# A delta rule's inverse of 16x16 blocks by two blocks of 8 and a product below them

## The chip, the cores and the metric

The kernel runs on one core of a Trainium2 chip. The metric is the device time of one execution of the whole program, in microseconds (us). TensorE is PE in the rows (PEld its weight loads), VectorE is DVE, ScalarE is ACT, GpSimd is POOL, and SyncE (SP) issues the DMAs of the weights.

## The reference, cut to what matters

Two residual blocks run one after the other on 256 tokens of width 1024. The first has two layers; each layer mixes tokens by three linear recurrences (RWKV-7, gated linear attention, gated DeltaNet), with feed-forward networks around them. Two of the three are delta rules, which are computed in chunks of 64 tokens; a chunk needs the inverse of a unit lower triangular 64x64 matrix per head. In the reference of the gated DeltaNet it is seen at once:

```python
decay = jnp.exp(jnp.where(causal, g[..., :, None] - g[..., None, :], -jnp.inf))
kb = k * beta[..., None]
lower = jnp.where(strict, jnp.einsum('bhnid,bhnjd->bhnij', kb, k) * decay, 0.0)
eye = jnp.eye(C, dtype=lower.dtype)
t_inv = lax.linalg.triangular_solve(eye + lower, jnp.broadcast_to(eye, lower.shape),
                                    left_side=True, lower=True)
u = t_inv @ (v * beta[..., None])
w = t_inv @ (kb * jnp.exp(g)[..., None])
```

C is 64, and with 4 heads and 4 chunks there are 16 such matrices. RWKV-7 is written as a scan over tokens, which the kernel computes in chunks of 64 in the same way, with 8 heads and so 32 matrices. `causal` is the lower triangle with its diagonal, `strict` the one without.

## The kernel before

**Weights.** All weights are streamed. A tile of 128x1024 (`wr`) comes by a DMA from SP, ACT casts it to its upper part `wh` (L81, CAST), DVE takes the rest as `wl` (L82), and each product is three passes on PE: L105, L106 and L108 where the output is transposed (128x256 in one pass), L184, L185 and L186 where it isn't (128x512). These passes are called fill below: they don't depend on the delta rules and can stand anywhere between their steps.

**Order.** Each engine runs its instructions in one fixed order, which the scheduler of the language sets when the program is built, from costs that it holds for each instruction; at run time semaphores only make an engine wait. So when an instruction's cost changes in the source, the order of all engines is made anew, and fill may come to stand ahead of a step or behind it.

**The inverse.** It runs four times in an execution: after the projections of RWKV (function `rw_inverse`) and in the middle of the gated DeltaNet (function `gd_mid`), in each of the two layers. The four places are called rw0, gd0, rw1 and gd1 here; they begin at about 285, 401, 1133 and 1249 us of the span. At rw0 and rw1 two groups of 16 matrices are inverted one after the other (two calls of `inv64`), at gd0 and gd1 one group. The steps:

- `inv_put` (L431) copies the 16x16 diagonal blocks of all matrices into a stage `stg`, by ACT (L440) and POOL (L438).
- `inv16` (L442) brings one block of 16x16 to each of the 128 partitions: a transposition on DVE (L449, tile `iA`), then a choice by a mask (L451, L452, tile `ia`). The inverse `ix` starts as the unit matrix and is filled row by row by forward substitution: for i from 1 to 15 a multiplication of i x i elements (L458, tile `ip`) and a sum over one of their axes (L459). Each step needs the one before. Two ACTIVATE on ACT (L462) spread the result, and a transposition (L464, tile `iB`) brings it back.
- `inv64` (L467) copies the blocks to the diagonal of 64x64 matrices, `z0` (tile `iz`), by four copies on ACT (L476, 32x256 elements each). From there it is PE's: inverses of 16 become inverses of 32 and then of 64 by masked products (L496) with DVE and ACT between them (L480, L491, L505, L507, L515, L519). PE's first product of the group, pc<-iz,NT at rw0 and rw1 and pc<-iz,int at gd0 and gd1, waits for the four copies.

In `gd_mid` (L850) the matrices are made ready first: the exponent of the decays is in `dd` (tile `gdd`, from ACT L869), and for each head and half of the tokens DVE multiplies `dd` by a number per partition (L876), then by the two masks (L878, L879, tile `gac`), then by the products from PE (L880 into `nt`, tile `int`, and L881 into `at`, tile `gat`). Lines L740 to L761 are the gated DeltaNet's convolution, work of ACT, DVE and PE that lies beside rw0 and rw1 (L744 on DVE, L757 on ACT, L760 on PE); L713 to L723 are the end of RWKV, beside gd0 and gd1, of which L714, L715 and L718 are POOL's and L721 and L722 are PE's.

Of the kernel before, what the change touches and what calls it, by code (L numbers as in the profile page):

```python
# [13 lines left out]
AF = mybir.ActivationFunctionType  # L14
ALU = mybir.AluOpType
# [390 lines left out]
class Mix(Core):  # L406
# [35 lines left out]
    def inv16(self, stg):  # L442

        nc = self.nc
        V = nc.vector
        sel = [self.cc("sel")[:, i:i + 1] for i in range(2)]
        fl = lambda z: z.rearrange("p a h u -> p a (h u)")
        at = self.t([P, 16, 32], "iA")
        V.transpose(at, fl(stg))  # L449
        a = self.t([P, 16, 16], "ia")  # L450
        V.tensor_scalar_mul(a, at[:, :, 0:16], sel[0])  # L451
        V.scalar_tensor_tensor(a, at[:, :, 16:], sel[1], a, ALU.mult, ALU.add)  # L452
        x = self.t([P, 16, 16], "ix")
        nc.gpsimd.memset(x, 0.0)
        nc.gpsimd.memset(x.rearrange("p a b -> p (a b)")[:, 0:256:17], 1.0)
        pr = self.t([P, 16, 16], "ip")
        for i in range(1, 16):
            V.tensor_tensor(pr[:, :i, :i], x[:, :i, :i], a[:, i, :i].rearrange("p (s o) -> p s o", o=1).broadcast_to([P, i, i]), ALU.mult)  # L458
            V.tensor_reduce(x[:, i, :i], pr[:, :i, :i].rearrange("p s c -> p c s"), mybir.AxisListType.X, ALU.add)  # L459
        e = self.t([P, 16, 32], "iA")  # L460
        for h in range(2):
            nc.scalar.activation(e[:, :, 16 * h:16 * h + 16], x.rearrange("p t s -> p s t"), AF.Identity, scale=sel[h])  # L462
        o = self.t([P, 16, 2, 16], "iB")
        V.transpose(fl(o), e)  # L464
        return o

    def inv64(self, nt, b, u0, xb):  # L467
# [5 lines left out]
        for q in range(4):  # L473
            r, c = slice(32 * q, 32 * q + 32), 32 * (q % 2)
            o = z0[r, :, c:c + 32].rearrange("p u (h a) -> p u h a", h=2)
            nc.scalar.copy(o, b[r, :, :, u0:u0 + 8].rearrange("p a h u -> p u h a"))  # L476
# [373 lines left out]
    def gd_mid(self):  # L850
# [4 lines left out]
        nk, sc = self.gnk, self.gsc  # L855
        for t in range(2):
# [5 lines left out]
        for t in range(2):  # L862
# [7 lines left out]
            for h in range(4):  # L870
# [5 lines left out]
                V.tensor_scalar_mul(dd[:, h], dd[:, h], nk[:, t, h:h + 1])  # L876
                d2 = self.t([P, 2, P], "gac", bufs=2, pool=self.gw)
                V.scalar_tensor_tensor(d2[:, 0], dd[:, h], -1.0, self.cc("mstr"), ALU.mult, ALU.mult)  # L878
                V.tensor_tensor(d2[:, 1], dd[:, h], self.cc("minc"), ALU.mult)  # L879
# [1251 lines left out]
```

## Time and profile before

| | |
|---|---|
| median of 3 runs | 2793.95 us (2792.52 to 2794.89) |
| profiled execution, its own time | 2792.3 us |
| span of the profile, from its first to its last instruction | 2790.5 us |
| granted TensorE clock, mean | 0.989 |
| PE busy | 2704.3 us, 97% of the span |
| DVE busy | 1885.5 us, 68% |
| ACT busy | 1300.7 us, 47% |
| POOL busy | 201.7 us, 7% |

Between the span and the execution's own time lie 1.8 us. In the rows a duration in us stands behind the start, "x3" is a count, and brackets at a row's end give the time that the engine stood idle just before and the instruction whose end it waited for. In the table by stretches "PEclk" is the clock granted to TensorE, as a share of 2.4 GHz: 1.00 is 2.4 GHz and 0.50 is 1.2 GHz.

### The profile page before, as it was taken

What the parts mean: (1) busy time and instruction counts of PE and PEld (TensorE: products, weight loads), DVE (VectorE), ACT (ScalarE), POOL (GpSimd) and SP (SyncE); (2) the same over time, 40 slices, a digit from 0 to 9 for tenths busy, and PEclk for the clock granted to TensorE, in tenths of its full rate; (3) what the DMA queues carried; (4) which work ended last, traced back from release to release, by engine and by line L of the source; (5) the groups of instructions that cost most, each with busy time, mean ns of one, the idle gap of its engine ahead of it and who ended that gap; (6) DMA issues with size and microseconds to landing.
All of it is one profiled execution on the core that took longest, in us unless ns stands there. A gap on an engine that the chain in (4) does not pass through costs nothing.

```text
span 2790.5 us, 47540 instructions
## 1 busy us (share of the span) xinstructions
PE 2704.3 (97%) x18676; PEld 2389.5 (86%) x18676; DVE 1885.5 (68%) x3852; ACT 1300.7 (47%) x2040; POOL 201.7 (7%) x332
## 2 busy tenths in 40 slices
PE   8999999999999999999999999999999999999998
PEld 8988877669988988887678986798999888898897
DVE  6658885876667658886777657775444337799764
ACT  5536543535444536643445534563333226565553
POOL 0000220020000001221010002200000001000000
PEclk9999999999999999999999999999999999999999
DMA  8654333376666554433376556112232323214564
GB/s 291 195 183 147 122 131 106 137 265 191 194 221 227 192 178 159 144 106 124 105 277 206 187 180 225 51 46 76 91 99 99 121 98 114 76 60 154 190 194 151
DMA packets 116799, 426.62 MB, mean 153 GB/s; under 512 B 13392, under 2 KB 13904, under 8 KB 115552
## 3 DMA queue, kind: packets, MB, share of 16 engines
q1 hardware_dynamic: 114960, 419.01, 45.0%
q0 software_dynamic: 1472, 4.51, 0.5%
q8 instruction: 147, 2.41, 0.4%
q14 instruction: 76, 0.62, 0.1%
q10 hardware_dynamic: 144, 0.07, 0.0%
HBM read 420.36 MB, written 3.18 MB: 152 GB/s over the span
## 4 chain that ended last, share of the span: by engine, by line
PE 83%; DVE 11%; ACT 3%; issue 2%; DMA 1%; POOL 0%; DVEq 0%; POOLq 0%; SPq 0%; ACTq 0%
PE ps L105 13%; PE ps L106 12%; PE ps L108 12%; PE ps L185 10%; PE ps L184 10%; PE ps L186 10%; DVE wl L82 2%; PE pc L496 2%; PE pt L252 2%; PE pc L1432 1%; PE pc L1686 1%; PE pt L1670 1%; PE pt L1873 1%; PE pc L667 1%; ACT wh L81 1%
## 5 line engine op out<-in xcount | busy, mean ns | idle before, releaser
L82 DVE TENSOR_TENSOR wl<-wr,wh 128x1024 fp32r<-128x1024 f32 x658 | 810.2, 1234 | 498.8 <-issue 180.6
L81 ACT CAST wh<-wr 128x1024 fp32r<-128x1024 f32 x658 | 687.7, 1048 | 641.1 <-PE ps L186 282.1
L105 PE MATMUL ps<-xh,wh 128*128 128x256 f32 x3280 | 920.6, 282 | 8.5 <-ACT xh L256 4.9
L106 PE MATMUL ps<-xh,wl 128*128 128x256 f32 x3280 | 914.8, 280 | 0.7 <-DVE wl L82 0.7
L108 PE MATMUL ps<-xl,wh 128*128 128x256 f32 x3168 | 882.3, 279 | 0.1
L105 PEld LDWEIGHTS ps<-xh,wh 128*128 128x128 f32 x3280 | 621.3, 190 | 20.7 <-ACT xh L256 7.8
L106 PEld LDWEIGHTS ps<-xh,wl 128*128 128x128 f32 x3280 | 620.4, 189 | 6.2 <-issue 4.2
L108 PEld LDWEIGHTS ps<-xl,wh 128*128 128x128 f32 x3168 | 595.2, 188 | 4.2 <-issue 3.2
L184 PE MATMUL ps<-wh,xh 128*128 128x512 f32 (+1 forms) x624 | 244.8, 395 | 2.3 <-ACT hq L1787 1.5
L185 PE MATMUL ps<-wl,xh 128*128 128x512 f32 (+1 forms) x624 | 245.2, 393 | 0.2 <-DVE wl L82 0.2
L186 PE MATMUL ps<-wh,xl 128*128 128x512 f32 (+1 forms) x624 | 243.1, 391 | 0.0
L184 PE MATMUL ps<-wh,hh 128*128 128x512 f32 (+1 forms) x616 | 227.7, 370 | 0.1
L186 PE MATMUL ps<-wh,hl 128*128 128x512 f32 (+1 forms) x616 | 227.2, 369 | 0.0
L185 PE MATMUL ps<-wl,hh 128*128 128x512 f32 (+1 forms) x616 | 226.8, 368 | 0.0
L184 PEld LDWEIGHTS ps<-wh,xh 128*128 128x128 f32 x624 | 117.2, 188 | 35.5 <-issue 4.5
L185 PEld LDWEIGHTS ps<-wl,xh 128*128 128x128 f32 x624 | 117.6, 188 | 24.7 <-issue 1.7
L186 PEld LDWEIGHTS ps<-wh,xl 128*128 128x128 f32 x624 | 117.4, 188 | 23.3 <-issue 0.7
L184 PEld LDWEIGHTS ps<-wh,hh 128*128 128x128 f32 x616 | 115.7, 188 | 21.6 <-DVE g L159 0.5
L186 PEld LDWEIGHTS ps<-wh,hl 128*128 128x128 f32 x616 | 115.6, 188 | 21.1
L185 PEld LDWEIGHTS ps<-wl,hh 128*128 128x128 f32 x616 | 115.8, 188 | 20.7
L156 ACT ACTIVATE th<-ps 128x256 f32<-128x256 f32 x154 | 59.3, 385 | 150.2 <-PE ps L108 140.5
L160 ACT CAST hh<-g 128x256 fp32r<-128x256 f32 x154 | 62.6, 406 | 115.7 <-DVE g L159 115.7
(568 smaller groups left out, 3707.6 us busy)
## 6 DMA issues: line engine op xcount, KB each, us to landing
wr<-in_up SPq DMA_DIRECT2D x264, 512.0 KB, 4.2
wr<-in_down SPq DMA_DIRECT2D x132, 512.0 KB, 3.4
wr<-in_wtm SPq DMA_DIRECT2D x72, 512.0 KB, 3.4
wr<-in_wfm SPq DMA_DIRECT2D x62, 512.0 KB, 3.3
fr<-in_ada SPq DMA_DIRECT2D x23, 1024.0 KB, 5.6
dz<-in_ada SPq DMA_DIRECT2D x13, 1024.0 KB, 8.1
wr<-in_wbr SPq DMA_DIRECT2D x24, 512.0 KB, 4.1
wr<-in_whfm SPq DMA_DIRECT2D x24, 512.0 KB, 3.4
```

The lines of the kernel that those rows point to most:

```text
L81: on_act = nc.scalar.copy(hi, raw)
L82: on_dve = nc.vector.tensor_tensor(lo, raw, hi.bitcast(F32), ALU.subtract)
L105: nc.tensor.matmul(o, hi[:, w], xh[:, k], start=k == 0, stop=False)
L106: nc.tensor.matmul(o, lo[:, w], xh[:, k], start=False, stop=False)
L108: nc.tensor.matmul(o, hi[:, w], xl[:, k], start=False, stop=k == nk - 1)
L156: nc.scalar.activation(th, pa[:, :T], AF.Tanh, scale=0.5)
L160: nc.scalar.copy(hh[:, m], g)
L184: nc.tensor.matmul(o, xh[:, k, s], h, start=first, stop=False)
L185: nc.tensor.matmul(o, xh[:, k, s], l, start=False, stop=False)
L186: nc.tensor.matmul(o, xl[:, k, s], h, start=False, stop=end)
L252: nc.tensor.transpose(pt[:, j, t * P:t * P + P], self.cols(src(t), t, k + j), self.ident)
L496: nc.tensor.matmul(ps[:, 64 * u:64 * u + 64], lhs[:, u], rhs[:, u], start=True, stop=True)
```

## The change

The solver for a block of 16 is split into its two diagonal blocks of 8, an upper one and a lower one. Both are solved at once by forward substitution in 7 steps instead of 15 (now L462 and L463, 2 x i x i elements each). The block below the diagonal of the inverse follows by two products of 8x8 matrices, each a multiplication of 512 elements (L467) and a sum over 8 of them (L469). `ia` and `ix` are kept in rows of 272 so that one view can step over the two diagonal blocks. Of the two spreading operations the second moves from ACT to DVE (L478). Of the four copies into `z0` two move from ACT to POOL (L494; ACT's are L496 now). In `gd_mid` the multiplication of `dd` by the number per partition is gone (8 instructions at each of gd0 and gd1); the two mask operations take that number as their scalar instead (L899, L900), one of them with its sign turned, which one small instruction per layer makes (L877).

```diff
@@ -447,19 +447,35 @@
         fl = lambda z: z.rearrange("p a h u -> p a (h u)")
         at = self.t([P, 16, 32], "iA")
         V.transpose(at, fl(stg))
-        a = self.t([P, 16, 16], "ia")
+        two = lambda z: z.rearrange("p (b z) -> p b z", z=136)[:, :, 0:P].rearrange("p b (s c) -> p b s c", c=16)[:, :, :, 0:8]
+        full = lambda z: z[:, 0:256].rearrange("p (a b) -> p a b", b=16)
+        af, xf = self.t([P, 272], "ia"), self.t([P, 272], "ix")
+        a, ad, x, xd = full(af), two(af), full(xf), two(xf)
         V.tensor_scalar_mul(a, at[:, :, 0:16], sel[0])
         V.scalar_tensor_tensor(a, at[:, :, 16:], sel[1], a, ALU.mult, ALU.add)
-        x = self.t([P, 16, 16], "ix")
-        nc.gpsimd.memset(x, 0.0)
-        nc.gpsimd.memset(x.rearrange("p a b -> p (a b)")[:, 0:256:17], 1.0)
-        pr = self.t([P, 16, 16], "ip")
-        for i in range(1, 16):
-            V.tensor_tensor(pr[:, :i, :i], x[:, :i, :i], a[:, i, :i].rearrange("p (s o) -> p s o", o=1).broadcast_to([P, i, i]), ALU.mult)
-            V.tensor_reduce(x[:, i, :i], pr[:, :i, :i].rearrange("p s c -> p c s"), mybir.AxisListType.X, ALU.add)
+        nc.gpsimd.memset(xf, 0.0)
+        nc.gpsimd.memset(xf[:, 0:256:17], 1.0)
+        pr = self.t([P, 8, 8, 8], "ip")
+        for i in range(1, 8):
+            m = pr[:, 0:2, :i, :i]
+            V.tensor_tensor(m, xd[:, :, :i, :i], ad[:, :, i, :i].rearrange("p b (s o) -> p b s o", o=1).broadcast_to([P, 2, i, i]), ALU.mult)
+            V.tensor_reduce(xd[:, :, i, :i], m.rearrange("p b s c -> p b c s"), mybir.AxisListType.X, ALU.add)
+        def product(out, l, r):
+            V.tensor_tensor(pr, l.rearrange("p i (s o) -> p i s o", o=1).broadcast_to([P, 8, 8, 8]),
+                            r.rearrange("p (o s) c -> p o s c", o=1).broadcast_to([P, 8, 8, 8]), ALU.mult)
+            V.tensor_reduce(out, pr.rearrange("p i s c -> p i c s"), mybir.AxisListType.X, ALU.add)
+        w = a[:, 0:8, 8:]
+        product(w, a[:, 8:, 0:8], x[:, 0:8, 0:8])
+        product(x[:, 8:, 0:8], x[:, 8:, 8:], w)
         e = self.t([P, 16, 32], "iA")
-        for h in range(2):
-            nc.scalar.activation(e[:, :, 16 * h:16 * h + 16], x.rearrange("p t s -> p s t"), AF.Identity, scale=sel[h])
+        xt = x.rearrange("p t s -> p s t")
+        nc.scalar.activation(e[:, :, 0:16], xt, AF.Identity, scale=sel[0])
+        V.tensor_scalar_mul(e[:, :, 16:], xt, sel[1])
         o = self.t([P, 16, 2, 16], "iB")
         V.transpose(fl(o), e)
         return o
@@ -473,7 +489,11 @@
         for q in range(4):
             r, c = slice(32 * q, 32 * q + 32), 32 * (q % 2)
             o = z0[r, :, c:c + 32].rearrange("p u (h a) -> p u h a", h=2)
-            nc.scalar.copy(o, b[r, :, :, u0:u0 + 8].rearrange("p a h u -> p u h a"))
+            i = b[r, :, :, u0:u0 + 8].rearrange("p a h u -> p u h a")
+            if q % 2:
+                nc.gpsimd.tensor_copy(o, i)
+            else:
+                nc.scalar.copy(o, i)
 
         def turned(z, tag):
             o = self.t([P, 8, 64], tag)
@@ -853,6 +873,8 @@
         V, G = nc.vector, nc.gpsimd
         be, g, eg = self.gdec
         nk, sc = self.gnk, self.gsc
+        nkn = self.t([P, 2, 4], "gnkn")
+        V.tensor_scalar_mul(nkn, nk, -1.0)
         for t in range(2):
             v = self.vb[:, t].rearrange("p (h c) -> p h c", h=4)
             G.tensor_tensor(v, v, be[:, t].rearrange("p (h o) -> p h o", o=1).broadcast_to([P, 4, P]), ALU.mult)
@@ -873,10 +895,9 @@
                 nc.tensor.matmul(ps[:, 0:P], k, sc["kb"][:, h, t * P:t * P + P], start=True, stop=True)
                 nc.tensor.matmul(ps[:, P:T], k, sc["qq"][:, h, t * P:t * P + P], start=True, stop=True)
 
-                V.tensor_scalar_mul(dd[:, h], dd[:, h], nk[:, t, h:h + 1])
                 d2 = self.t([P, 2, P], "gac", bufs=2, pool=self.gw)
-                V.scalar_tensor_tensor(d2[:, 0], dd[:, h], -1.0, self.cc("mstr"), ALU.mult, ALU.mult)
-                V.tensor_tensor(d2[:, 1], dd[:, h], self.cc("minc"), ALU.mult)
+                V.scalar_tensor_tensor(d2[:, 0], dd[:, h], nkn[:, t, h:h + 1], self.cc("mstr"), ALU.mult, ALU.mult)
+                V.scalar_tensor_tensor(d2[:, 1], dd[:, h], nk[:, t, h:h + 1], self.cc("minc"), ALU.mult, ALU.mult)
                 V.tensor_tensor(nt[:, 4 * t + h], ps[:, 0:P], d2[:, 0], ALU.mult)
                 V.tensor_tensor(at[:, 4 * t + h], ps[:, P:T], d2[:, 1], ALU.mult)
         self.gat = at
```

In the changed kernel's numbering PE's products of the inverse are L516 (before: L496), the transposition back is L480 (L464), the convolution's lines are 20 higher, and so on.

**On PE at rw0**, around the first product of the first group. The tiles named `ps` and `w...` are fill. Before, the product stands inside the passes over one weight tile of the kind L105:

```order
L105 MATMUL ps_3996<-xh_2232,wh_3997 128x256
L106 MATMUL ps_3996<-xh_2232,wl_3998 128x256
L108 MATMUL ps_3996<-xl_2233,wh_3997 128x256
L496 MATMUL pc_3387<-iz_565_3373,NT_353_2315 128x64 x8
L105 MATMUL ps_3996<-xh_2232,wh_3997 128x256
```

Of the change:

```order
L184 MATMUL ps_3861<-wh_3917,xh_2232 128x512
L185 MATMUL ps_3861<-wl_3918,xh_2232 128x512
L516 MATMUL pc_3375<-iz_565_3361,NT_353_2315 128x64 x8
L780 MATMUL pt_3851<-cst,gth_3847 128x2 x2
L186 MATMUL ps_3861<-wh_3917,xl_2233 128x512
L184 MATMUL ps_3862<-wh_3917,xh_2232 128x512
L185 MATMUL ps_3862<-wl_3918,xh_2232 128x512
L186 MATMUL ps_3862<-wh_3917,xl_2233 128x512
L105 MATMUL ps_3937<-xh_2232,wh_3938 128x256
```

The product stands earlier now: 1918 passes of fill lie ahead of it since the program's start, where 1964 did, so 46 passes moved behind it (4 of the kind L184 to L186, 42 of the kind L105 to L108). One pair of the convolution's products (L780) moved behind it too. At rw1 the same count went from 6302 to 6231, which is 71 passes.

**On DVE at rw0**, the end of the solver. Before, its last steps are:

```order
L459 TENSOR_REDUCE ix_3333<-ip_3336 128x14
L82 TENSOR_TENSOR wl_4047<-wr_4048,wh_4046 128x1024
L458 TENSOR_TENSOR ip_3336<-ix_3333,ia_3330 128x15x15
L459 TENSOR_REDUCE ix_3333<-ip_3336 128x15
L464 STREAM_TRANSPOSE iB_3370<-iA_3367 128x512
```

Of the change:

```order
L467 TENSOR_TENSOR ip_3336<-ia_3330,ix_3331 128x512
L764 SCALAR_TENSOR_TENSOR gac_3842<-gxi_3839,vt_2281,gac_3842 128x256
L469 TENSOR_REDUCE ia_3330<-ip_3336 128x8x8
L781 TENSOR_SCALAR gss_3664<-pt_3804 128x2
L467 TENSOR_TENSOR ip_3336<-ix_3331,ia_3330 128x512
L764 SCALAR_TENSOR_TENSOR gac_3842<-gxi_3839,vt_2281,gac_3842 128x256
L469 TENSOR_REDUCE ix_3331<-ip_3336 128x8x8
L764 SCALAR_TENSOR_TENSOR gac_3842<-gxi_3839,vt_2281,gac_3842 128x256
L478 TENSOR_SCALAR iA_3355<-ix_3331,cst 128x16x16
L82 TENSOR_TENSOR wl_3918<-wr_3919,wh_3917 128x1024
L480 STREAM_TRANSPOSE iB_3358<-iA_3355 128x512
```

Other work still stands between the steps. From the first multiplication to the last sum there were 7 L82, 9 L744, 4 L756 and 4 L761 among the 30 steps of the solver; now there are 3 L82, 9 L764, 3 L776 and 3 L781 (the same lines, renumbered) among its 18.

**On POOL at gd0**, where the stage is filled. Before:

```order
L714 TENSOR_TENSOR ytm_2280<-ytm_2280,rt_3668 128x512
L715 TENSOR_TENSOR ytm_2280<-ytm_2280,rt_3668 128x512
L718 TENSOR_TENSOR ytm_2280<-ytm_2280,vnat_2279 128x512
L438 COPY stg_4584<-int_4480 32x2x16x8 x2
L714 TENSOR_TENSOR ytm_2280<-ytm_2280,rt_3668 128x512
L715 TENSOR_TENSOR ytm_2280<-ytm_2280,rt_3668 128x512
L718 TENSOR_TENSOR ytm_2280<-ytm_2280,vnat_2279 128x512
```

Of the change:

```order
L734 TENSOR_TENSOR ytm_2280<-ytm_2280,rt_3656 128x512
L735 TENSOR_TENSOR ytm_2280<-ytm_2280,rt_3656 128x512
L738 TENSOR_TENSOR ytm_2280<-ytm_2280,vnat_2279 128x512
L734 TENSOR_TENSOR ytm_2280<-ytm_2280,rt_3656 128x512
L735 TENSOR_TENSOR ytm_2280<-ytm_2280,rt_3656 128x512
L738 TENSOR_TENSOR ytm_2280<-ytm_2280,vnat_2279 128x512
L438 COPY stg_4566<-int_4470 32x2x16x8 x2
L494 COPY iz_810_4605<-iB_4602 32x8x32 x2
```

Both sets of RWKV's end now stand ahead of the copies into the stage; at gd1 the stage's copies still stand between the two sets. On PE the distance between the last product that `gd_mid` reads (L874, now L896) and the first product of the inverse went from 90 passes of fill to 68 at gd0, and from 91 to 70 at gd1. At gd0 the count ahead of the inverse's first product is 2258 in both kernels, so there it is the step ahead that moved later.

## Rows read from the trace of the kernel before

**Rows 1.** The page's busy times, and its chain by engine.

```profile
PE 2704.3 (97%) x18676; PEld 2389.5 (86%) x18676; DVE 1885.5 (68%) x3852; ACT 1300.7 (47%) x2040; POOL 201.7 (7%) x332
...
PE 83%; DVE 11%; ACT 3%; issue 2%; DMA 1%; POOL 0%; DVEq 0%; POOLq 0%; SPq 0%; ACTq 0%
```

**Rows 2.** PE's waits, the two largest: what for, us in total, times, longest.

```profile
PE pc L496 <- ACT iz L476: 14.3, 4, 4.7
PE pt L252 <- DVE x L300: 10.6, 9, 2.7
```

**Rows 3.** PE's timeline at rw0, gd0, rw1, gd1: the inverse's first product.

```profile
315.09 2.29 PE L496 MATMUL pc<-iz,NT 128*128 128x64 f32 x16 [2.55 <-ACT iz L476]
...
431.83 3.64 PE L496 MATMUL pc<-iz,int 128*128 128x64 f32 x16 [4.44 <-ACT iz L476]
...
1163.80 1.97 PE L496 MATMUL pc<-iz,NT 128*128 128x64 f32 x16 [2.57 <-ACT iz L476]
...
1278.00 3.65 PE L496 MATMUL pc<-iz,int 128*128 128x64 f32 x16 [4.74 <-ACT iz L476]
```

**Rows 4.** Stretches: us, busy (x) of PE, PEld, DVE, ACT, POOL, PEclk, DMA share, GB/s.

```profile
315.00:322.00 7.00, 6.91 (x47) 6.94 (x48) 4.06 (x7) 4.56 (x8) 0.28 (x2) 0.76 0.36 111
431.80:446.00 14.20, 14.17 (x70) 13.65 (x71) 6.57 (x13) 2.78 (x6) 1.44 (x4) 0.61 0.01 1
1163.80:1170.00 6.20, 6.20 (x54) 6.20 (x55) 4.22 (x7) 5.10 (x10) 0.44 (x1) 1.00 0.29 88
1278.00:1292.00 14.00, 14.00 (x69) 13.49 (x70) 6.24 (x12) 2.76 (x6) 1.44 (x4) 0.59 0.00 0
```

**Rows 5.** DVE's timeline at rw0: the solver, and what stands beside it.

```profile
297.83 0.22 DVE L458 TENSOR_TENSOR ip<-ix,ia 128x64 f32<-128x64 f32 x1
...
298.30 0.25 DVE L459 TENSOR_REDUCE ix<-ip 128x8 f32<-128x64 f32 x1
...
308.07 1.21 DVE L82 TENSOR_TENSOR wl<-wr,wh 128x1024 fp32r<-128x1024 f32 x1
309.20 0.39 DVE L458 TENSOR_TENSOR ip<-ix,ia 128x225 f32<-128x225 f32 x1
309.63 0.55 DVE L459 TENSOR_REDUCE ix<-ip 128x15 f32<-128x225 f32 x1
311.67 0.71 DVE L464 STREAM_TRANSPOSE iB<-iA 128x512 f32<-128x512 f32 x1 [1.49 <-ACT iA L462]
```

**Rows 6.** The solver's steps alone, a stretch for each place: us, DVE busy (count), clock, DMA.

```profile
287.90:310.20 22.30, 8.47 (x30) 1.00 0.58 189
409.60:426.90 17.30, 9.41 (x30) 1.00 0.55 177
...
1255.20:1272.60 17.40, 10.43 (x30) 1.00 0.54 175
```

**Rows 7.** ACT's timeline at gd0, the copies.

```profile
429.16 2.53 ACT L476 COPY iz<-iB 32x256 f32<-32x256 f32 x4
```

**Rows 8.** POOL's copies by form: ns, least/median/most.

```profile
L438 POOL COPY stg<-int x4: 653/1174/1700, 403.6 to 1250.9; 32x256 f32<-32x256 f32 x4
```

**Rows 9.** PE's fill at rw0, one pass after the other.

```profile
306.42 0.40 PE L185 MATMUL ps<-wl,xh 128*128 128x512 f32 x1
306.65 0.40 PE L186 MATMUL ps<-wh,xl 128*128 128x512 f32 x1
...
307.58 0.28 PE L105 MATMUL ps<-xh,wh 128*128 128x256 f32 x1
307.69 0.28 PE L106 MATMUL ps<-xh,wl 128*128 128x256 f32 x1
```

**Rows 10.** DVE's timeline at gd0, beside work of POOL.

```profile
417.83 0.92 DVE L458 TENSOR_TENSOR ip<-ix,ia 128x100 f32<-128x100 f32 x1
...
420.47 1.99 DVE L82 TENSOR_TENSOR wl<-wr,wh 128x1024 fp32r<-128x1024 f32 x1
```

**Rows 11.** DVE's scaling of dd by form: ns, least/median/most.

```profile
L876 DVE TENSOR_SCALAR gdd<-gdd,gnk x16: 276/279/286, 393.6 to 1247.4; 128x128 f32<-128x128 f32 x16
```

## The prediction

> **What bounds it.** The page comes first [rows 1]: PE is busy for 97% of the span and holds 83% of the chain that ended last, DVE 11%. So work taken from DVE or ACT counts only where PE stands idle for it, or where its clock falls. The view of PE's waits says where that is: the largest wait is the inverse's first product, for the copies into z0, 14.3 us in four waits [rows 2]; next come nine waits for a normalization's transposition, which this change leaves alone. PE's timeline gives the four: 2.55 us at rw0, 4.44 at gd0, 2.57 at rw1, 4.74 at gd1 [rows 3].
>
> Each wait can leave a second cost, the granted clock behind it [rows 4]. Over the stretch that follows the product at rw1 it is 1.00, that is 2.4 GHz all along; behind rw0's it is 0.76 in the mean of 7 us, behind gd0's 0.61 of 14.2 us, behind gd1's 0.59 of 14 us, since for a part of each it was at 0.50, 1.2 GHz. PE works throughout these stretches, so the loss is length times what is missing: 7 x 0.24 = 1.7 us at rw0, 14.2 x 0.39 = 5.5 at gd0, 14 x 0.41 = 5.7 at gd1. It shows in the product itself: its 16 matmuls take 1.97 us at rw1, 2.29 at rw0, 3.64 and 3.65 at gd0 and gd1 [rows 3]. Waits and clock together make 14.3 + 12.9 = 27 us, 1% of the execution: the ceiling of what this change can give at these places.
>
> **The sum, part by part.** The prediction is made against the profiled execution, 2792.3 us, and then set on the median, which is 1.65 us above it.
>
> *The solver.* Multiplying goes from 0.22 us at 64 elements to 0.39 at 225, summing from 0.25 to 0.55 [rows 5], that is 1.06 and 1.86 ns per element above about 0.15 and 0.13 us. The seven steps on pairs have 280 elements in all: 7 x 0.15 + 0.30 = 1.4 us and 7 x 0.13 + 0.52 = 1.4 us. A multiplication of 512 elements is then 0.69 us and its sum 1.08, and two products are 3.5 us. Together 6.3 us, where the 30 steps take 8.47, 9.41 and 10.43 us [rows 6]. The extrapolation to 512 is the unknown price here: not under 0.39 and 0.55 us (the 225 elements), hardly over twice my values, which would eat the whole gain. I take the straight line, since the steps follow one. So DVE saves only some 2 us of its own work; what shortens the chain is that fewer other instructions stand between 18 steps than between 30.
>
> *rw0.* In the new order of DVE 4 of 7 L82 are gone from between the steps; each takes 1.13 us to the next start [rows 5], so 4.5 us; one L756 and one L761 less give 0.4. With 2.2 of the solver itself, the last sum, which ended at 310.2 (309.63 + 0.55), ends at about 303.1. L478 adds 0.4 (256 elements on the line above), an L82 behind it 1.1, the transposition 0.7: iB at 305.3 instead of 312.4. Then two copies on POOL beside two on ACT. ACT needs 2.53 us for four [rows 7], so 1.3 for two; POOL's copies of the same shape took 0.65 to 1.70 us, 1.17 in the middle [rows 8], so 2.35 for two, which is about what ACT's four took. iz is ready at 307.6. PE comes sooner as well, by the order of the two: 4 passes at 0.23 us and 42 at 0.115 [rows 9] moved behind the product, 5.8 us, so that it arrives where two thirds of the last such tile are done, at 306.65. The wait is 1.0 us instead of 2.55, bounds 0.3 and 2. I take the half clock as gone, since a wait of 2.57 us left the clock at 1.00 at rw1: 1.55 + 1.7 = **3.2 us**.
>
> *rw1.* The first product moved ahead by 71 passes, 8.2 us, so PE arrives at 1153 plus some 0.7 for one convolution product that waits behind ACT's spread. The chain loses by the order five L82 (5.7 us), 2 us of steps and 0.8 of idle time, and is ready at some 1155.5 instead of 1163.8. The wait is about 2.2 instead of 2.57: **0.4 us**, bounds 0 and 1.5.
>
> *gd0.* The steps there go from 17.2 us to about 10: 9.41 become 6.3 [rows 6], by the order six L82 become three (3.4 us), and small work of RWKV's end stands before them. The contention of DVE with POOL ends too, since both of POOL's sets now precede the stage: a step took 0.92 us beside it, an L82 1.99 [rows 10]. But 22 passes at 0.23 us, 5.1 us, no longer lie between what starts the chain and the product, and one of L741 and L742's two pairs moved half behind it, 0.5. So the wait loses 7.0 - 5.6 = 1.4 and is 3.0. Of the 5.5 us of clock I take 1.5 as saved: 3.0 lies between the waits that left it low for long (4.44) and for a short time (2.55). **2.9 us**, bounds 0 and 7.
>
> *gd1.* The same, but POOL's set stays beside the steps, and 21 passes are missing: the chain loses 5.3 us, PE's cover 4.85. **0.5 us**, bounds 0 and 3.
>
> *The scaling of dd.* Eight instructions of 0.28 us [rows 11] go at each of gd0 and gd1, about 1.6 us of DVE each with overlap; PE waits there for under 1 us in each layer, so I count **0.4 us** together. The sign's instruction costs nothing that PE waits for.
>
> The sum is 3.2 + 0.4 + 2.9 + 0.5 + 0.4 = 7.4 us: 2784.9 for an execution like the profiled one, 2786.5 for the median.
>
> **A rule against it.** While one of POOL's operations ran, a solver's step of 100 elements took 0.92 us and an L82 1.99 [rows 10], against 0.39 for 225 elements and 1.21 [rows 5]; and POOL's own copies vary from 0.65 to 1.70 us [rows 8]. The Trainium skill, "SBUF — State Buffer", section "SBUF: two separate sides", says why: DVE and GpSimd take a shared pair of ports in turn, the first holds it for its whole instruction, and the other stands still. By it a copy that meets an L82 would end up to 1.2 us late, and rw0's sum would be up to 1.2 us worse per copy; the trace agrees in kind. The sum above uses the middle row.
>
> **Rivals.**
> - *The waits move along.* The scheduler moved PE's products forward by what it thought that the chain would save (5.8 us at rw0, 8.2 at rw1, 5.1 and 4.85 at the others). If the chip saves just that, each wait and each clock stays, and only the dd instructions and a piece of rw0 are left: 0 to 3 us, 2792.4. For it speaks that the four distances all shrank by nearly what DVE saves; against it that the scheduler can't know of POOL's interference that ends at gd0.
> - *The clock stays high.* If the shorter waits at gd0 and gd1 leave the clock at 1.00, as rw1's did, the 5.5 and 5.7 us come back, less the 1.5 counted: 7.4 + 4.0 + 5.7 = 17.1 us, 2776.9. For it: rw1 waits 2.57 us and keeps 1.00. Against: both waits would have to lose nearly 2 us, and behind rw0's 2.55 the clock did fall.
> - *Slower: PE comes early and the chain doesn't.* The place is rw0 and rw1, where PE's product moved furthest. If 512-element steps cost twice the line (3.5 us more) or POOL's copies are held by DVE (1.2 each), iz is late by 3 us or more: waits of 4 to 5 us, and behind each a clock as after gd0's 4.44. At rw0 1.5 us more of wait and 3.8 of clock (5.5 for 1.7), at rw1 2.3 and 5.5; 13 us, less some 3.5 that the other two still give: 2803. It decides from a wait of about 4 us at these two, where I have 1.0 and 2.2.
> - *The change doesn't do what it says*: no path shortens because ACT's casts set the time at which the copies start. Then nothing moves, 2794. ACT has 47% load [rows 1], so this is small.
>
> **Numbers.** Forecast 0.46, waits move along 0.20, clock stays high 0.18, slower 0.14, nothing 0.02. A change is told from none here beyond 0.2%, which is 5.6 us. The forecast's own range is 2782 to 2792, of which some 70% lies more than 5.6 us below the median. Faster: 0.46 x 0.7 + 0.18 = 0.50; slower: 0.14 and a little of the rest, 0.17; same: 0.33. The range takes in the larger gain and the slower case to a part: 2776 to 2798, which leaves out half of the slower case and the largest gains.
>
> **What would show it.** In the changed kernel's waits: the product's (now L516) for iz as 1.0, 3.0, 2.2 and 4.2 us; the clock at 1.00 behind rw0's; L467 at 0.7 us and L469 at 1.1; POOL's copies into iz at 1.2 each. I am wrong if L469 is over 1.5, if a wait at rw0 or rw1 is over 3 us, or if the clock falls for as long as before at gd0 although the wait is shorter; and if waits appear elsewhere, as in RWKV's chain, between whose steps somewhat less fill stands now.

## The result, and the profile of the changed kernel

The changed kernel takes 2812.85 us (median of 9 runs, 2809.82 to 2821.13); the kernel before, run beside it, 2794.89 us (9 runs). The ratio is 1.0061, its 95% interval 1.0047 to 1.0075: slower by 0.6%, some 17 us, where 7 us less were forecast and 2798 was the end of the range.

The page's busy times [rows 1]:

```profile
PE 2718.2 (97%) x18676; PEld 2400.0 (85%) x18676; DVE 1887.1 (67%) x3794; ACT 1290.1 (46%) x2024; POOL 208.7 (7%) x344
```

PE runs the same 18676 matmuls, yet is busy 13.9 us longer. Its idle time, the span less its busy time, went from 86.2 us (2790.5 - 2704.3) to 91.8 (2810.0 - 2718.2). So of the 19.5 us between the two spans 5.6 are new waiting, and 13.9 are more busy time for the same matmuls. DVE has 1.6 us more, though 58 instructions less.

PE's waits, those that changed [rows 2]: what for, us in total, times, longest:

```profile
PE pc L516 <- POOL iz L494: 9.9, 4, 5.2
PE pc L1453 <- DMA fr<-in_ada: 5.7, 2, 3.6
...
PE pt L780 <- ACT gth L777: 3.5, 3, 2.0
```

In the kernel before, L780 was L760:

```profile
PE pt L760 <- ACT gth L757: 1.5, 2, 1.1
```

The inverse's product waits 9.9 us instead of 14.3, as it was meant to. But a product of the doses now waits 5.7 us for its DMA. (A dose is a product over weights that come by a DMA of their own into `fr`, between the other work: L1453, the same as L1432 before.) No wait for `fr` was listed before; in the new order the two products that wait stand 21 and 22 passes of fill earlier. L780 waits 2.0 us more, and L895, a product of the gated DeltaNet, waits 1.9 us where the same line (L873) waited 0.7.

The same at its places, from PE's timeline [rows 3]:

```profile
307.58 2.00 PE L516 MATMUL pc<-iz,NT 128*128 128x64 f32 x16 [1.13 <-POOL iz L494]
...
375.73 1.06 PE L1453 MATMUL pc<-fr,adac 128*32 128x512 f32 x8 [2.10 <-DMA fr<-in_ada]
...
432.45 3.52 PE L516 MATMUL pc<-iz,int 128*128 128x64 f32 x16 [2.31 <-POOL iz L494]
...
1157.13 0.61 PE L780 MATMUL pt<-cst,gth 128*128 128x2 f32 x4 [2.00 <-ACT gth L777]
...
1160.42 2.00 PE L516 MATMUL pc<-iz,NT 128*128 128x64 f32 x16 [1.20 <-POOL iz L494]
...
1232.86 1.94 PE L1453 MATMUL pc<-fr,adac 128*32 128x512 f32 x8 [3.60 <-DMA fr<-in_ada]
...
1292.85 3.67 PE L516 MATMUL pc<-iz,int 128*128 128x64 f32 x16 [5.22 <-POOL iz L494]
```

These are the first products at rw0 (307.58), gd0 (432.45), rw1 (1160.42) and gd1 (1292.85), the two doses, and at 1157.13 the convolution's product that stands ahead of rw1's. The third cost is seen in the clock, stretch by stretch [rows 4] (the number third from the end is PEclk):

```profile
309.00:314.00 5.00, 5.00 (x29) 4.62 (x27) 2.36 (x4) 2.79 (x4) 0.00 (x0) 0.66 0.52 171
337.00:341.00 4.00, 4.00 (x23) 4.00 (x23) 1.68 (x4) 0.42 (x1) 0.11 (x1) 0.57 0.19 75
431.80:450.00 18.20, 17.07 (x68) 14.62 (x69) 7.80 (x14) 3.43 (x7) 2.38 (x7) 0.53 0.07 25
1186.00:1194.00 8.00, 8.00 (x44) 7.88 (x42) 2.53 (x7) 0.73 (x2) 0.10 (x1) 0.57 0.21 66
1231.00:1239.00 8.00, 6.14 (x20) 3.65 (x21) 2.30 (x14) 1.33 (x3) 0.00 (x0) 0.57 0.54 192
1289.00:1310.00 21.00, 17.15 (x68) 14.84 (x68) 11.02 (x18) 5.90 (x10) 3.96 (x8) 0.51 0.15 49
```

PE's busy time times what is missing from 1.00 is what a stretch costs. The sum over the whole span, worked out in stretches of 1 us, is 24.4 us before and 37.4 after, so the clock is 13.0 of the 13.9 us. At rw0 it is the same 1.7 us; new are 1.7 us at 337 (the second group's end) and 3.4 at 1186 (RWKV's chain), both without any wait ahead, and 2.6 at 1231, behind the dose. At gd0 5.5 became 8.2, at gd1 5.7 became 8.5.

### The profile page after: what moved, and what is told of

Its sections match the earlier page's. It is cut to its first block, busy times and chain, and to the rows that moved or that the text cites. A ratio compares the mean times of both kernels' runs of the same rounds, so it can differ in the third digit from the quotient of the medians.

```text
span 2810.0 us, 47484 instructions
## 1 busy us (share of the span) xinstructions
PE 2718.2 (97%) x18676; PEld 2400.0 (85%) x18676; DVE 1887.1 (67%) x3794; ACT 1290.1 (46%) x2024; POOL 208.7 (7%) x344
## 4 chain that ended last, share of the span: by engine, by line
PE 82%; DVE 11%; ACT 2%; issue 2%; DMA 1%; POOL 1%; DVEq 0%; POOLq 0%; ACTq 0%; SPq 0%
PE ps L105 12%; PE ps L106 12%; PE ps L108 12%; PE ps L184 10%; PE ps L186 9%; PE ps L185 9%; DVE wl L82 2%; PE pc L516 2%; PE pt L252 1%; PE pc L1707 1%; PE pc L1453 1%; PE pt L1691 1%; PE pt L1894 1%; DMA fr<-in_ada 1%; PE pc L687 1%
## 5 line engine op out<-in xcount | busy, mean ns | idle before, releaser
L82 DVE TENSOR_TENSOR wl<-wr,wh 128x1024 fp32r<-128x1024 f32 x658 | 813.4, 1239 | 507.0 <-issue 189.4
L105 PE MATMUL ps<-xh,wh 128*128 128x256 f32 x3280 | 922.6, 283 | 9.0 <-ACT xh L256 5.4
L108 PE MATMUL ps<-xl,wh 128*128 128x256 f32 x3168 | 885.2, 280 | 0.4 <-DVE xl L263 0.3
L105 PEld LDWEIGHTS ps<-xh,wh 128*128 128x128 f32 x3280 | 622.2, 190 | 22.3 <-ACT xh L256 8.4
L108 PEld LDWEIGHTS ps<-xl,wh 128*128 128x128 f32 x3168 | 596.9, 189 | 4.3 <-issue 2.4
L184 PE MATMUL ps<-wh,xh 128*128 128x512 f32 (+1 forms) x624 | 245.8, 397 | 2.3 <-ACT hq L1808 1.5
L186 PE MATMUL ps<-wh,xl 128*128 128x512 f32 (+1 forms) x624 | 244.3, 393 | 0.0
L184 PE MATMUL ps<-wh,hh 128*128 128x512 f32 (+1 forms) x616 | 227.9, 370 | 0.1
L186 PE MATMUL ps<-wh,hl 128*128 128x512 f32 (+1 forms) x616 | 227.5, 369 | 0.0
L184 PEld LDWEIGHTS ps<-wh,xh 128*128 128x128 f32 x624 | 117.9, 189 | 36.4 <-issue 5.3
L186 PEld LDWEIGHTS ps<-wh,xl 128*128 128x128 f32 x624 | 118.3, 190 | 23.2 <-issue 0.7
L184 PEld LDWEIGHTS ps<-wh,hh 128*128 128x128 f32 x616 | 115.9, 188 | 21.4 <-DVE g L159 0.5
L186 PEld LDWEIGHTS ps<-wh,hl 128*128 128x128 f32 x616 | 115.8, 188 | 21.0
```

The costliest lines, as they stand in the source:

```text
L82: on_dve = nc.vector.tensor_tensor(lo, raw, hi.bitcast(F32), ALU.subtract)
L105: nc.tensor.matmul(o, hi[:, w], xh[:, k], start=k == 0, stop=False)
L108: nc.tensor.matmul(o, hi[:, w], xl[:, k], start=False, stop=k == nk - 1)
L184: nc.tensor.matmul(o, xh[:, k, s], h, start=first, stop=False)
L186: nc.tensor.matmul(o, xl[:, k, s], h, start=False, stop=end)
```

## The experiments

**Theory A**: the new instructions cost what they were priced at; the time goes to the order that the scheduler made of them. It took the inverse's products at rw0 and rw1 46 and 71 passes ahead, and what followed, RWKV's chain, the doses and the gated DeltaNet, was left with less fill, waits and a low clock. **Theory B**: the new instructions cost more than priced, POOL's copies beside DVE above all.

All ratios are to the kernel before, run beside each, with 95% intervals; "us" is the ratio less one, times 2795. "Clock" is the granted clock, the mean over all runs of a kernel; for the kernel before, beside e1 to e14, it is 0.9868 to 0.9872. A thousandth of it is 2.8 us of a span of 2795 us, by which the share of the clock in a difference is estimated below. One profile can be off: the profiled execution before had 0.989.

| kernel | ratio | interval | us | clock |
|---|---|---|---|---|
| the change | 1.0061 | 1.0047 to 1.0075 | +17 | 0.9827 |
| e1: RWKV's places alone | 1.0032 | 1.0021 to 1.0043 | +9 | 0.9859 |
| e2: the gated DeltaNet's alone | 1.0010 | 0.9999 to 1.0020 | +3 | 0.9879 |
| e3: solver alone | 1.0049 | 1.0033 to 1.0065 | +14 | 0.9850 |
| e4: split copies alone | 1.0047 | 1.0032 to 1.0062 | +13 | 0.9840 |
| e5: change, RWKV's products tied back | 0.9982 | 0.9970 to 0.9994 | -5 | 0.9871 |
| e12: e5 again | 0.9980 | 0.9971 to 0.9989 | -6 | 0.9875 |
| e6: change, gate pair tied ahead | 1.0016 | 1.0004 to 1.0028 | +4 | 0.9866 |
| e7: change, dose tied later | 1.0042 | 1.0027 to 1.0057 | +12 | 0.9842 |
| e8: before, RWKV's end written earlier | 1.0020 | 1.0003 to 1.0037 | +6 | 0.9874 |
| e9: e5 and e6 together | 1.0020 | 1.0011 to 1.0030 | +6 | 0.9837 |
| e10: e9, copies on ACT | 0.9993 | 0.9984 to 1.0002 | -2 | 0.9865 |
| e11: e4, gate pair tied ahead | 0.9994 | 0.9983 to 1.0004 | -2 | 0.9885 |
| e13: e5, copies on ACT | 1.0002 | 0.9992 to 1.0012 | +1 | 0.9865 |
| e14: e9, fill between the products | 0.9983 | 0.9972 to 0.9994 | -5 | 0.9875 |

### e1 to e4: the change in parts

e1 keeps the old solver, copies and `gd_mid` at gd0 and gd1; e2 keeps the old solver and copies at rw0 and rw1. In short:

```diff
-        self.gX = self.inv64(nt, self.inv16(stg), 0, ...)
+        self.gX = self.inv64(nt, self.inv16_old(stg), 0, ...)
...
-            if q % 2:
+            if q % 2 and any(nt is m for m in self.NT):
                 nc.gpsimd.tensor_copy(o, i)
```

> The new solver and the split copies at RWKV's two places (rw0, rw1) alone; the gated DeltaNet's places keep the old solver, four ACT copies and the scaling of dd. Theory A, the loss comes from the order that the scheduler makes at rw0 and rw1 (the inverse's products 46 and 71 passes earlier, RWKV's chain and the first dose after it with less fill, the dose's product ahead of its DMA, the gated DeltaNet's inverse with fewer passes of cover): this kernel has the same order there as the whole change (1918 and 6231 passes ahead of the first product), so it is slower than before by 12 to 22 us, with the dose's wait of 2 and 3.6 us and the low clock at 337 and 1186 us. Theory B, the loss is the price of the new instructions themselves (POOL's copies, sums of 512 elements): each place pays its part, so about half, 6 to 10 us.

> The new solver, the split copies and the folded scaling at the gated DeltaNet's two places (gd0, gd1) alone; rw0 and rw1 as before. Here the order ahead of the gated DeltaNet stays as before (1964 and 6302 passes ahead of RWKV's first product), and the first product of the inverse at gd0 and gd1 stands 83 passes behind its inputs (before: 90 and 91). Theory A: faster than before, by 4 to 14 us, because the chain of the inverse is 7 us shorter while the cover is only 7 passes (1.6 us) smaller; wait for iz under 1.5 us at both. Theory B: slower by 6 to 10 us.

e1 is 9 us slower: that is theory B's number (6 to 10) and under theory A's 12 to 22, though both waits of the doses that theory A named are in it (2.0 and 3.6 us). e2 is some 3 us slower, neither the gain of theory A nor the loss of theory B, and its waits for iz at gd0 and gd1 are 5.2 and 6.7 us where theory A had under 1.5. So both theories fail in part here. The two parts together make 12 us against 17, which these intervals don't tell apart.

e3 takes `inv16` alone from the change, e4 the copies alone:

```diff
-            nc.scalar.copy(o, b[r, :, :, u0:u0 + 8].rearrange("p a h u -> p u h a"))
+            i = b[r, :, :, u0:u0 + 8].rearrange("p a h u -> p u h a")
+            if q % 2:
+                nc.gpsimd.tensor_copy(o, i)
+            else:
+                nc.scalar.copy(o, i)
```

> The new solver at all four places, with the old scaling of dd and all four copies on ACT. Theory A: the order at rw0 and rw1 is nearly that of the whole change (1921 and 6234 passes), so slower than before by 8 to 20 us though no copy runs on POOL. Theory B with POOL's copies as the price: within 5 us of before or faster, and faster than the whole change by over 10 us.

> Only the split of the four copies between ACT and POOL, old solver and old scaling. The order moves by 5 or 6 passes. Theory A: within 4 us of before. Theory B with POOL's copies as the price: slower by 8 us or more.

e3 comes out as theory A has it: 14 us without a copy on POOL. e4 doesn't: 13 us, theory B's number, though the first products at rw0 and rw1 move by only 5 and 6 passes. But PE's order changed at gd0 and gd1 too. The stretches behind the product there:

```profile
434.00:456.00 22.00, 19.38 (x79) 16.70 (x79) 9.63 (x17) 5.25 (x10) 2.65 (x6) 0.53 0.07 25
1288.00:1309.00 21.00, 18.87 (x75) 16.21 (x75) 8.72 (x16) 4.86 (x10) 2.49 (x6) 0.51 0.06 22
```

PE is busy for 19.38 and 18.87 us at half clock, 9.4 and 9.3 us of cost by the finer stretches, where before had 5.5 and 5.7; its waits for iz are 13.7 us, hardly less than 14.3. What stands behind the product there, from PE's timeline at gd0:

```profile
436.15 3.65 PE L501 MATMUL pc<-iz,int 128*128 128x64 f32 x16 [4.51 <-POOL iz L478]
439.73 2.07 PE L727 MATMUL pt<-gx,misc 32*128 32x512 f32 x2
```

In the kernel before, L496's product at 431.83 comes when all four of RWKV's gate products (L721, L722) are done. In e4 the last pair member (L727 here) stands behind it. The fill that follows, passes over `bh`, is made from RWKV's output, which needs that pair. The change has the same row, L742. PE's timeline of the changed kernel at gd0, from the end of that product on:

```profile
435.90 2.07 PE L742 MATMUL pt<-gx,misc 32*128 32x512 f32 x2
...
438.81 3.52 PE L516 MATMUL pc<-iym,ixb 128*128 128x64 f32 x16
...
443.65 0.79 PE L184 MATMUL ps<-wh,bh 128*128 128x512 f32 x1 [0.47 <-ACT bh L256]
444.24 3.51 PE L516 MATMUL pc<-iz,int 128*128 128x64 f32 x16
447.51 0.78 PE L185 MATMUL ps<-wl,bh 128*128 128x512 f32 x1
```

From 432.45 to 447.51 PE has small products, transpositions and one pass of fill (443.65), all at half clock: L516's 16 take 3.5 us instead of 1.9. So a second part of theory A, which e6, e11 and e14 test: what counts at gd0 and gd1 is the fill behind the product.

### e5: RWKV's products tied back

The kernel keeps every pass of fill in a list, and the inverse's products in another, and uses `behind` (L88, an order without a semaphore of its own between two instructions):

```diff
+        g = self.invs[-2:]
+        self.behind(g[0][0], self.fills[(1963, 6301)[l]])
+        self.behind(g[1][0], self.fills[(1999, 6341)[l]])
```

> All instructions of the change, but the first products of the inverse at rw0 and rw1 are tied behind the same pass of fill as in the kernel before (46 and 71 passes later than the change has them). Theory A, it is the order that the scheduler made, not its instructions: RWKV's chain and the doses get their fill back, 79 passes lie between the gated DeltaNet's inputs and its inverse instead of 68 and 10 to 16 more behind its first product, so faster than the change by 12 to 25 us, that is 8 us faster to 4 us slower than before; no wait for iz at rw0 and rw1, no wait for a dose over 1 us. Theory B, the new instructions and POOL's part beside DVE: still 9 to 17 us slower than before.

-5 us, and -6 when it was run again (e12): 22 us faster than the change with all of its instructions. PE's timeline at gd0, and the product at gd1:

```profile
422.15 1.97 PE L518 MATMUL pc<-iz,int 128*128 128x64 f32 x16 [1.91 <-POOL iz L496]
423.93 0.52 PE L187 MATMUL ps<-wh,xl 128*128 128x512 f32 x1
...
1270.10 3.08 PE L518 MATMUL pc<-iz,int 128*128 128x64 f32 x16 [2.80 <-ACT iz L498]
```

and the stretches there:

```profile
420.00:436.00 16.00, 14.09 (x85) 11.97 (x84) 12.10 (x19) 5.33 (x8) 8.79 (x12) 0.89 0.30 99
1268.00:1284.00 16.00, 13.90 (x67) 11.49 (x68) 10.53 (x16) 6.26 (x9) 8.68 (x11) 0.79 0.22 68
```

PE still waits 1.91 and 2.80 us, but passes over `xh` and `xl`, which need nothing of RWKV, follow from 423.93 on, eight of them before the next product; the clock's mean is 0.89 and 0.79 over 16 us. rw0 and rw1 have no wait for iz left, no dose waits over 1 us. This is theory A's strongest run: the instructions are the change's, and as many passes stand ahead of RWKV's first products as before.

What it gained is waiting and clock together. PE's idle time in its profile is 79.8 us, against 91.8 in the change and 86.2 before, and its clock is 0.9871, some 12 us of the 22 over the change's 0.9827. Against before the clock is the same: the 5 to 6 us that it is ahead are less waiting, which is what the change was made for.

### e6 and e11: the gate pair ahead

```diff
+            last = nc.tensor.matmul(pg, self.misc[0:32, s], self.gx[0:32, 512:], start=False, stop=True)
+            for m in self.imm[:1]:
+                self.behind(m, last)
```

`imm` holds the products of the inverse at gd0 or gd1. e6 does this to the change, e11 to e4.

> The change, with one thing: the second pair of L741 and L742 (RWKV's gate) is tied ahead of the inverse's first product at gd0 and gd1, as it stands in the kernel before. In the trace of the change the low clock there lasts 18 and 21 us (13 and 15 before) because the fill behind the product needs RWKV's output, and that needs this pair. Theory A: the low clock loses 2 to 3 us of cost at each, so 4 to 6 us faster than the change, 10 to 14 slower than before. Theory B: no difference to the change, within 2 us.

> The split copies alone (old solver, old scaling), which were 13 us slower than before, with the second gate pair tied ahead of the inverse's first product at gd0 and gd1. Theory A: those 13 us were that pair's place, so now within 5 us of before. Theory B, POOL's copies: still 8 us or more slower.

e6 gains 13 us on the change, over twice the forecast, and e11 gains 15 on e4 and is level with before. PE's order differs from e4's only at gd0 and gd1, in that pair and in what the scheduler put behind it; copies and solver are the same. So the 13 us of e4 were the place of that pair. The clock has most of it, some 11 of the 13 us and 13 of the 15. In e6's stretches (the last two are gd0 and gd1, to be held against 18.2 and 21 us in the change) the low clock is shorter:

```profile
1150.00:1161.00 11.00, 10.27 (x37) 8.45 (x36) 5.16 (x7) 3.59 (x5) 2.12 (x2) 0.53 0.54 166
430.00:441.00 11.00, 11.00 (x55) 10.71 (x54) 5.67 (x11) 2.87 (x6) 1.83 (x6) 0.53 0.03 9
1283.00:1295.00 12.00, 7.96 (x42) 7.81 (x42) 7.74 (x13) 5.51 (x9) 2.12 (x2) 0.57 0.27 87
```

The cost at gd0 and gd1 is 5.1 and 3.4 us, where the change had 8.2 and 8.5. The first row is rw1, where e6 lost 4.8 us and e1 4.6, the change nothing; see the last section.

### e7: the dose later

```diff
+        d = [m for s, m in self.doz if s[0] == 'd' and s[1:].isdigit()]
+        self.behind(d[1 if l == 0 else self.nd + 1], self.fills[(2097, 6421)[l]])
```

`doz` holds the doses' products with the place in the program that made them.

> The change, with one thing: the dose whose product waits 2.1 us (at 376 us) and 3.6 us (at 1233 us) for its DMA is tied 15 and 32 passes of fill further back. Theory A: these two waits go, and with them the low clock behind the second (2.6 us): 5 to 8 us faster than the change, 9 to 13 slower than before. Rival: PE only waits for the same thing later, since the gated DeltaNet's decays on DVE are late as well (they end the stage's chain): within 3 us of the change.

5 us faster than the change, but the intervals overlap, so a gain isn't shown. The edit also ties the wrong product: the one that it moves 15 and 32 passes is the dose's product ahead of the one that waits, which moved with it by 14 and 16. PE's waits for iz and for the dose:

```profile
PE pc L518 <- POOL iz L496: 12.3, 4, 5.1
...
PE pc L1462 <- DMA fr<-in_ada: 3.0, 2, 2.1
```

2.7 us of the dose's waits went, all of it in layer 1 (3.60 to 0.89 us; in layer 0 it is 2.08 for 2.10), and 2.4 came back in front of the inverse: the rival has the waits. What stayed gained in this profile is the clock behind the second dose, 2.6 us, which fell no more.

### e8: RWKV's end written earlier

```diff
+                    self.rw_post()
                     with new("mj") as self.mx:
                         self.gd_mid()
...
-                    self.rw_post()
```

> The kernel before, with one thing: the end of RWKV (L697, rw_post) is written ahead of the gated DeltaNet's middle, so that its output, and the fill that needs it, comes sooner; 8 passes of that fill then stand ahead of the inverse's first product at gd0 and 3 at gd1, and 5 to 12 between its products instead of 0, 3, 8. Theory A: the wait of 4.4 and 4.7 us shrinks and the clock comes back behind it, 5 to 15 us faster than before, if the solver isn't delayed by more than the cover won. Rival: DVE sets the stage's length, and its work is the same: within 4 us of before.

Slower by 6 us: a miss for theory A, and outside the rival's 4 us too. Its ten times lie between 2793.6 and 2810.6 us, and the profiled one is the longest. Three of PE's waits in it:

```profile
PE pc L496 <- ACT iz L476: 6.2, 4, 2.6
...
PE pt L873 <- DVE ytm L723: 4.7, 2, 3.2
...
PE ps L184 <- ACT bh L256: 4.2, 2, 3.7
```

The wait for iz is 6.2 us instead of 14.3, but PE now waits 4.7 us ahead of products of `gd_mid` that come only after L723 (DVE's part of RWKV's end, now ahead of the gated DeltaNet) and 4.2 for `bh`. Together that is 15.1 us: writing the work in another order moved the wait.

### e9, e10, e12 to e14: which wait, and which copies

e9 has both ties; e10 and e13 put all copies on ACT, in e9 and in e5.

> The change with both ties: RWKV's products behind the fill of the kernel before, and the second gate pair ahead of the inverse's first product at gd0 and gd1. All fill of the stage (95 and 92 passes instead of 79 and 78) then lies between the gated DeltaNet's inputs and its inverse. Theory A: the waits of 1.9 and 2.8 us at gd0 and gd1 that were left with the first tie alone fall under 0.5 and no long low clock follows: 3 to 8 us faster than with the first tie alone, 8 to 13 us faster than before. Rival: the clock falls behind the product without any wait, since only small products follow it: within 2 us of the first tie alone.

e9 should have been the fastest and is 6 us slower than before. PE's timeline at gd0 and the stretches at gd0 and gd1:

```profile
427.37 2.00 PE L518 MATMUL pc<-iz,int 128*128 128x64 f32 x16
430.23 0.77 PE L1491 MATMUL pt<-cst,row 128*128 128x128 f32 x4 [0.86 <-DVE ytm L749]
...
432.88 3.65 PE L518 MATMUL pc<-iym,ixb 128*128 128x64 f32 x16 [0.18 <-DVE mod L1493]
```

```profile
430.00:445.00 15.00, 14.01 (x58) 12.40 (x58) 7.03 (x14) 1.74 (x5) 1.83 (x6) 0.54 0.05 20
1283.00:1298.00 15.00, 13.96 (x56) 12.40 (x57) 6.96 (x14) 1.67 (x5) 1.83 (x6) 0.54 0.05 21
```

There is no wait for iz: the product runs at 427.37 in 2.00 us, at 2.4 GHz. Then come only small products, with pauses of 0.86 and 0.58 us for RWKV's output, and the clock falls all the same; the next 16 take 3.65 us. All fill over `xh` was used up ahead. The cost is 6.4 and 6.5 us, more than e5's 1.7 and 3.4 there: the mechanism that the rival named, though e9 is 11 us slower than e5 and not within 2. PE's idle time is the same 79.8 us in both. e14 ties 17 passes of that fill in between; what follows is the scheduler's again (RWKV's products over `row` and `ytm` and the passes over `bh` now stand behind most or all of the inverse):

```diff
+        for i in range(3):
+            self.behind(self.fills[(2234, 6558)[l] + 8 * i], self.imm[8 * i + 7])
```

> As the kernel with both ties (e9), with one thing: the last 17 passes of fill are tied behind the products of the inverse at gd0 and gd1 (4 behind the first, 4 behind the second, 9 behind the third) instead of standing ahead of the first. So PE reaches the first product some 4 us sooner. Theory A, the clock stays low as long as small products follow each other, whether or not PE waited: the waits for iz come back, 2 to 4 us at each place, but the low clock there (6.4 and 6.5 us of cost in e9) falls to 4 or less: 2 to 8 us faster than e9 in all. Rival, waits decide: slower than e9 by 4 to 8 us.

It is 10 us faster than e9, more than theory A's 2 to 8. Waits came back, but in front of the product after the first, from PE's timeline:

```profile
431.61 2.73 PE L518 MATMUL pc<-iym,ixb 128*128 128x64 f32 x16 [2.26 <-DVE iym L528]
...
1283.55 3.65 PE L518 MATMUL pc<-iym,ixb 128*128 128x64 f32 x16 [3.08 <-DVE iym L528]
```

so PE waits more (81.1 us of idle time for 79.8) and the kernel is faster. By its profile the low clock cost 5.1 and 2.9 us there instead of 6.4 and 6.5; that is 5 of the 10 us. But the profiled execution took 2798.4 us, 6 more than e14's median, and lost 6.8 us to the clock in RWKV's chain from 340 us on. Over all runs the clock is 0.9875 for e9's 0.9837, which is some 10 us: the gain is the clock.

> As the kernel with both ties, with all four copies into z0 on ACT. The order on PE is the same pass by pass, so this prices POOL's copies alone. Theory A: POOL's two copies take as long as ACT's four and nothing waits for either, within 2 us of the kernel with both ties. Theory B: 4 us or more faster than with the copies on POOL.

> The kernel with only the first tie (RWKV's products back) once more, beside its twin with the copies on ACT. Theory A: again 2 to 8 us faster than before, since fill stands between the products of the inverse at gd0 and gd1. Rival, the first result was a lucky draw of the clock: within 2 us of before, as the kernel with both ties.

> The same tie with all four copies into z0 on ACT. PE's order is the same up to the gated DeltaNet's inverse, whose first product stands 2 or 3 passes later. Theory A (POOL's copies cost nothing by themselves; the 6 us between the two kernels with both ties were the clock at a few places): within 3 us of its twin. Theory B (POOL's copies cost 6 us): 4 to 9 us faster than its twin.

e10 is 7 us faster than e9, as theory B has it, but e13 is 6 us slower than its twin e12, which neither theory had. In the first pair PE's order differs by the place of one pair of the convolution's products (L780) alone. No wait for iz is left in either and PE's idle time is the same (79.8 and 80.1 us); the clock is 0.9865 for 0.9837, some 8 us. So the 7 us are no wait for a copy. Why the clock is lower with the copies on POOL stays open, but e10's timeline at gd0 shows that PE's order doesn't settle it:

```profile
426.40 2.00 PE L514 MATMUL pc<-iz,int 128*128 128x64 f32 x16
...
431.11 1.97 PE L514 MATMUL pc<-iym,ixb 128*128 128x64 f32 x16 [0.64 <-DVE mod L1489]
```

The order there is e9's and the pauses are of 0.70 and 0.64 us, yet nothing is lost to the clock, where e9 lost 6.4 us. In the second pair the order differs more: by L780, by 2 and 3 passes ahead of the gated DeltaNet's inverse, and in layer 0 by much of what follows up to about 560 us. There e13 waits: its idle time is 85.7 us for 79.0, 3.4 of it for the doses and 1.4 for iz. So no one price can be put on POOL's copies from these pairs; e11, with them, is level with before.

## Why the prediction was wrong

**Prices: right in the main.** DVE's timeline at rw0 [rows 5], and POOL's copies by form [rows 8]:

```profile
298.11 0.68 DVE L467 TENSOR_TENSOR ip<-ia,ix 128x512 f32<-128x512 f32 x1
...
299.11 1.17 DVE L469 TENSOR_REDUCE ia<-ip 128x64 f32<-128x512 f32 x1
...
304.43 0.71 DVE L480 STREAM_TRANSPOSE iB<-iA 128x512 f32<-128x512 f32 x1
```

```profile
L494 POOL COPY iz<-iB x12: 602/624/1508, 305.3 to 1291.3; 32x256 f32<-32x256 f32 x12
```

The copies at rw0, from the timelines of POOL, ACT and DVE:

```profile
305.27 2.25 POOL L494 COPY iz<-iB 32x256 f32<-32x256 f32 x2 [1.85 <-DVE iB L480]
305.35 1.32 ACT L496 COPY iz<-iB 32x256 f32<-32x256 f32 x2
305.36 1.70 DVE L82 TENSOR_TENSOR wl<-wr,wh 128x1024 fp32r<-128x1024 f32 x1
```

L467 took 0.68 us (0.69 forecast), L469 1.06 to 1.18 (1.08), L478 0.45 (0.4); the 18 steps were busy for 6.6 us at gd0 (6.3) and for 8.6 at gd1; iB was ready at 305.1 (305.3). POOL's copies took 0.62 us in the middle where 1.17 was taken, but the second at rw0 took 1.51 beside an L82, and that L82 1.70 where 1.2 is usual. So the two came to 2.25 us, close to the 2.35 forecast, by luck: one was cheaper and one dearer than the price. In kind this bears out the rule that was held against the copies, the Trainium skill's page "SBUF — State Buffer", section "SBUF: two separate sides", by which DVE and GpSimd take a shared pair of ports in turn. PE's wait hung on it: at rw0, rw1 and gd1 one of POOL's two copies took 1.50 us or a little more, and POOL was done 0.85, 0.93 and 0.46 us after ACT. That is 2.2 of the 9.9 us of waits, but little of the 17.

**Waits for iz: right at rw0 and gd0, close elsewhere.** 1.13 for 1.0 at rw0, 2.31 for 3.0 at gd0, 5.22 for 4.2 at gd1. At rw1 1.20, and 2.00 for the convolution's product ahead of it: 3.2 together. The prediction says 2.2 there, but its own numbers give 1.8 (ready at 1155.5, PE there at 1153.7), and 2.5 with the 0.7 for the convolution's product.

**The clock: the step that failed, by its sign.** 3.2 us were counted as saved, and 13.0 more were lost. "I take the half clock as gone" at rw0 failed: it fell behind a wait of 1.13 us as behind 2.55, 1.7 us. At gd0 1.5 us less were counted, with the wait as the measure ("3.0 lies between the waits"); 2.7 more were measured, though the wait halved. The step took the length of the wait as what decides. e9 shows it isn't: no wait for iz, and the clock falls; e14 shows longer waits with fill behind and a faster kernel. Nor does PE's order alone decide: e10 has e9's at gd0 and kept 2.4 GHz. What does stays open. That one of the two pairs of L741 and L742 had "moved half behind it" was seen, and priced at 0.5 us of cover; e6 and e11 put it at 13 and 15 us.

**What was moved: left out, the second step that failed.** The sum has the four places of the inverse and nothing between them. The passes that moved behind RWKV's product were counted as cover lost in front of it, not as fill missing behind: the dose that came ahead of its DMA (5.7 us of waits), L780 and L895 (3.2 us more), the clock in RWKV's chain. The last clause of the prediction named such waits and gave them no price. e5 shows the size of what hung on the moved products, waits and clock together: 22 us.

**The rivals.** The slower one had the place, rw0 and rw1, and the cause that PE comes earlier than it should, but its mechanism, waits of 4 to 5 us there, didn't happen: they were 1.1 and 3.2. Waits that move along were seen (e7, e8), but as waits for other things.

## What to carry to other kernels

Where a scheduler makes the order anew from its own costs, a saving in one stage can be spent by it at once: count, on the engine that bounds, not only the cover ahead of the shortened step but what fill is left behind it, up to the next stage, and look at every DMA, dose or output that the step now precedes. A wait can be cheaper than its cure: in e14 some full-width passes kept to follow the small matmuls cost 1.3 us of waiting and brought 10 us. If a change of instructions loses, tie the few moved ones back to their old neighbours before dropping it; here this turned 17 us of loss into 5 to 6 of gain (e5, e12).

## What the runs showed of the hardware that was not expected

The clock can fall behind small products without a long wait: in e9 at 430 us, after 16 matmuls of 128x64 that ran at 2.4 GHz. And it isn't fixed by PE's order alone, as e10 shows at the same place. The change's product at rw1 ran in 2.00 us behind a wait of 1.20; with the same order at this place e6's took 3.67 behind a wait of 0.73, from PE's timeline:

```profile
1152.61 3.67 PE L517 MATMUL pc<-iz,NT 128*128 128x64 f32 x16 [0.73 <-POOL iz L495]
```

In RWKV's chain of layer 1, with nothing waited for, e10 was at half clock for 25 us and e9, with the same order there, for 8, by their stretches:

```profile
1183.00:1208.00 25.00, 25.00 (x129) 21.79 (x128) 10.89 (x31) 6.15 (x15) 0.67 (x2) 0.52 0.19 64
```

```profile
1191.00:1199.00 8.00, 8.00 (x38) 5.98 (x37) 3.56 (x9) 2.10 (x5) 0.57 (x1) 0.57 0.33 124
```

What decides between these stays open; it makes single profiles differ by several us, which is why the verdicts above rest on all runs. The folded scaling of dd was not run alone.
